# Cutting both tables' loads and the last two positions' stores by partition in a rotary-embedding kernel

## The chip, the cores and the metric

One Trainium2 chip, of which the kernel uses one core. The metric is the device time of one execution in microseconds (us). Before the change it is 163.35 us, the median of three runs that lie between 163.29 and 163.39 us.

## What is computed

The reference rotates pairs of numbers. `x` is float32 of shape (batch 8, positions 2048, heads 8, 64); `cos` and `sin` are float32 tables of shape (2048, 32), shared by all batches and heads:

```
x1, x2 = x[..., :32], x[..., 32:]
out1 = x1 * cos - x2 * sin
out2 = x1 * sin + x2 * cos
out  = concatenate([out1, out2], axis=-1)
```

The input and the output are 33.55 MB each, each table is 0.26 MB. Nothing is reduced, so every byte of `x` comes in once and every byte of `out` goes out once.

## The kernel before, in words

**Tiling.** The 2048 positions of a batch are laid on the 128 partitions, 16 consecutive positions on each. One position is HD = 8 x 64 = 512 numbers, that is 2 KB per partition; a batch is a tile `xt` of 128 rows by 8192 numbers (32 KB per row, 4 MB). A UNIT is four positions: 128 x 2048 numbers, 1 MB. The tables `cos_sb` and `sin_sb` are 128 rows of 512 numbers, 2 KB per row.

**Loads.** `load(b)` (lines 64 to 70) issues the loads of batch b on SyncE's queue (SP). Batch 0 comes in three parts (1, 1 and 2 MB), and right after the first part the cos table is loaded (line 69); every other batch is one 4 MB load. The sin table is loaded first of all on ScalarE's queue (ACT, line 76). Five tiles rotate (NBUF = 5): the loads of batches 0 to 4 are asked for at once, and batch b + 5 is loaded into the tile of batch b when that batch's stores have landed.

**Work.** `rotate(b, lo, n)` works on one piece, in place. In the commonest form ("A") GpSimd (POOL) multiplies the swapped halves by the sin table and by its negative `nsin` (line 122, two instructions), VectorE (DVE) multiplies by the cos table (line 129) and adds the two products back into `xt` (line 136). In five pieces of the run (kinds "B" and "C") TensorE adds the products through an identity matrix and ScalarE copies the sum back (lines 143 to 165). ScalarE makes `nsin` from the sin table once, after a table load of its own (line 90), and a copy of the sin table for "C" (line 91); VectorE copies the cos table once (line 93).

**Stores.** `store(b, lo, n)` (lines 72 to 74) writes a finished part out: on ACT's queue for batches 0 to 6 and on SP's for the last batch. `pieces(b)` (lines 170 to 175) gives the pieces of work, `shares(b)` (lines 177 to 182) the parts that are stored. The last batch is worked in three UNITs and two pieces of two positions each, and stored as 2 UNITs, 1 UNIT and 1 UNIT: the last store, 1 MB with rows of 8 KB, starts when the last piece is done.

**Order.** The order on each engine is the order of the program (`keep`). Every DMA signals on one of eight completion semaphores that are given out in turn, so a DMA that takes a semaphore up again waits first until that semaphore's DMA before it has landed. On the chip a DMA is carried by 16 DMA engines side by side; in the trace every DMA of this kernel has 16 landing marks, one for each of them, and it is complete with the last.

Of the kernel before, what the change touches and what calls it, by code (L numbers as in the profile page):

```python
# [10 lines left out]
def kernel(  # L11
# [7 lines left out]
    nc = tc.nc  # L19
    keep = tc.keep_in_program_order  # L20
# [5 lines left out]
    P = 128  # L26
    HD = H * D
    R = S // P
    ROW = R * HD
    UNIT = 4 * HD  # L30
    NBUF = 5
    C = 512
    last = B - 1

    xv = x.rearrange("b (q r) h d -> b q (r h d)", q=P)
    ov = out.rearrange("b (q r) h d -> b q (r h d)", q=P)
    cos_src = cos.rearrange("(q r) d -> q r d", q=P)
    sin_src = sin.rearrange("(q r) d -> q r d", q=P)
# [9 lines left out]
    cos_sb = const_pool.tile([P, R, Dh], f32, tag="cb")  # L48
    sin_sb = const_pool.tile([P, R, Dh], f32, tag="sb")
# [6 lines left out]
    xts = {}  # L56

    def spans(sizes):
        lo = 0
        for n in sizes:  # L60
            yield lo, n
            lo += n

    def load(b):
        xt = xpool.tile([P, ROW], f32, tag="xt", name=f"xt{b}")
        for lo, n in spans([UNIT, UNIT, 2 * UNIT] if b == 0 else [ROW]):
            keep(nc.sync.dma_start(out=xt[:, lo : lo + n], in_=xv[b, :, lo : lo + n]))
            if b == 0 and lo == 0:
                keep(nc.sync.dma_start(out=cos_sb, in_=cos_src))
        xts[b] = xt  # L70

    def store(b, lo, n):
        queue = nc.sync if b == last else nc.scalar
        keep(queue.dma_start(out=ov[b, :, lo : lo + n], in_=xts[b][:, lo : lo + n]))

    keep(nc.scalar.dma_start(out=sin_sb, in_=sin_src))
    for b in range(NBUF):
        load(b)

# [2 lines left out]
        out=eye,  # L82
        in_=eye,
# [93 lines left out]
    def shares(b):  # L177
        if b == 0:
            return [UNIT, UNIT, 2 * UNIT]
        if b == last:  # L180
            return [2 * UNIT, UNIT, UNIT]
        return [ROW]

    for b in range(B):
        done = 0
        outs = list(spans(shares(b)))
        for lo, n in spans(pieces(b)):
            rotate(b, lo, n)
            done = lo + n
            while outs and sum(outs[0]) <= done:  # L190
                store(b, *outs.pop(0))
        if b + NBUF <= last:
            load(b + NBUF)
# [30 lines left out]
```

## Time and profile before

| what | before |
|---|---|
| median of three runs | 163.35 us |
| the profiled execution, its own time | 163.35 us |
| its span, first to last instruction | 161.5 us |
| DVE busy | 140.1 us (87%) |
| POOL busy | 138.9 us (86%) |
| PE, PEld, ACT busy | 49.2, 18.5, 12.8 us |
| first packet of the first load begins | 1.75 us |
| first POOL product begins, first DVE product begins | 6.64 us, 7.79 us |
| last DVE sum ends | 152.2 us |
| last store issued, landed | 152.23 us, 160.71 us |
| bytes moved, mean rate over the span | 67.65 MB, 419 GB/s |
| DMA packets | 3458 |

Between the span and the execution's own time lie 1.85 us outside of the instructions. The busy shares are of the span. A "landing" is the moment at which the last of the 16 marks of a DMA is set. All times inside a run count from the span's start. The 40 digits of a row of the page stand for slices of 4.04 us.

### The profile page before, as it was taken

The page shows a single profiled execution, that of the slowest core. Times are in us where ns is not written, and L with a number is a line of the kernel's source. Part 1 is how long each engine was busy: PE and PEld are TensorE (multiplying, and loading weights), DVE is VectorE, ACT ScalarE, POOL GpSimd, SP SyncE. Part 2 cuts the span into 40 slices and gives each one's busy share as a digit, 9 for nine tenths or more (in the row PEclk, how much of TensorE's full clock was granted, in tenths as well). Part 3 has the DMA queues.
Part 4 walks back from the last instruction along what each step waited for, and adds up shares of the span by engine and source line. Part 5 has one row for each costly group of instructions (what it writes and reads, how often), then busy time and mean ns, then how long its engine had stood idle before and what let it go on. Part 6 is the DMA issues. An engine that isn't in the chain of part 4 may idle for free.

```text
span 161.5 us, 460 instructions
## 1 busy us (share of the span) xinstructions
PE 49.2 (30%) x80; PEld 18.5 (11%) x80; DVE 140.1 (87%) x66; ACT 12.8 (8%) x14; POOL 138.9 (86%) x70
## 2 busy tenths in 40 slices
PE   0000000597309770978039723973000000000000
PEld 0000000142004220323023302320000000000000
DVE  0297999999999999999999999999999999999600
ACT  3300000002200220021100220022000000000000
POOL 1399997999999999999994999999999999996000
PEclk9999999999975998589956995599655555555555
DMA  5999998998999999999999999999999999999994
GB/s 153 423 458 418 430 487 381 430 487 381 487 398 446 389 462 389 462 446 389 487 422 389 487 416 389 487 422 398 473 422 406 471 422 406 471 422 406 426 404 209
DMA packets 3458, 67.65 MB, mean 419 GB/s; under 512 B 384, under 2 KB 384, under 8 KB 640
## 3 DMA queue, kind: packets, MB, share of 16 engines
q1 hardware_dynamic: 2016, 38.01, 55.3%
q10 hardware_dynamic: 1440, 29.62, 42.8%
q14 instruction: 2, 0.02, 0.0%
HBM read 34.08 MB, written 33.55 MB: 419 GB/s over the span
## 4 chain that ended last, share of the span: by engine, by line
DVE 75%; POOL 9%; issue 6%; DMA 4%; DVEq 0%
DVE t L129 40%; DVE xt L136 33%; POOL t L122 9%; DMA sin_sb<-in_sin_dram 4%; DVE t L148 3%; DVEq L136 0%
## 5 line engine op out<-in xcount | busy, mean ns | idle before, releaser
L122 POOL TENSOR_TENSOR t<-xt,sin_sb 128x1024 f32<-128x1024 f32 (+1 forms) x32 | 71.2, 2226 | 8.5 <-DMA sin_sb<-in_sin_dram 5.3
L129 DVE TENSOR_TENSOR t<-xt,cos_ps 128x2048 f32<-128x2048 f32 (+1 forms) x34 | 73.4, 2166 | 0.8
L122 POOL TENSOR_TENSOR t<-xt,nsin 128x1024 f32<-128x1024 f32 (+1 forms) x32 | 71.3, 2228 | 0.0
L136 DVE TENSOR_TENSOR xt<-t,t 128x2048 f32<-128x2048 f32 (+1 forms) x29 | 62.2, 2145 | 4.2 <-POOL t L122 1.2
L143 PE MATMUL o<-t,eye 128*128 128x512 f32 x24 | 16.9, 797 | 23.1 <-DVE t L129 19.7
L160 PE MATMUL o<-t,eye 128*128 128x512 f32 x16 | 12.0, 842 | 37.9 <-DVE t L129 35.7
L144 PE MATMUL o<-t,eye 128*128 128x512 f32 x24 | 14.9, 709 | 0.0
L145 ACT COPY xt<-o 128x1024 f32<-128x1024 f32 x6 | 6.1, 1012 | 45.7 <-PE o L144 45.7
L143 PEld LDWEIGHTS o<-t,eye 128*128 128x128 f32 x24 | 5.5, 256 | 32.5 <-issue 26.6
L160 PEld LDWEIGHTS o<-t,eye 128*128 128x128 f32 x16 | 3.7, 256 | 43.4 <-issue 39.5
L165 ACT COPY xt<-o 128x1024 f32<-128x1024 f32 x4 | 4.0, 1012 | 47.8 <-PE o L161 47.8
L93 DVE COPY cos_ps<-cos_sb 128x512 f32<-128x512 f32 x1 | 0.7, 695 | 7.1 <-DMA cos_sb<-in_cos_dram 7.1
L144 PEld LDWEIGHTS o<-t,eye 128*128 128x128 f32 x24 | 5.6, 235 | 8.1 <-issue 8.1
L161 PE MATMUL o<-t,neye 128*128 128x512 f32 x8 | 6.2, 872 | 0.2
L148 DVE TENSOR_TENSOR t<-xt,sin_ps 128x2048 f32<-128x2048 f32 x2 | 4.6, 2280 | 0.0
L161 PE MATMUL o<-t,eye 128*128 128x512 f32 x8 | 4.1, 592 | 0.0
L161 PEld LDWEIGHTS o<-t,neye 128*128 128x128 f32 x8 | 2.1, 296 | 5.2 <-issue 3.6
L161 PEld LDWEIGHTS o<-t,eye 128*128 128x128 f32 x8 | 1.5, 190 | 1.9 <-issue 1.9
L90 ACT ACT_TABLE_LOAD x1 | 1.3, 1283 | 1.2 <-PEq L208 1.2
L90 ACT ACTIVATE nsin<-sin_sb 128x512 f32<-128x512 f32 x1 | 0.6, 630 | 4.1 <-DMA sin_sb<-in_sin_dram 4.1
L91 ACT COPY sin_ps<-sin_sb 128x512 f32<-128x512 f32 x1 | 0.6, 578 | 0.0
L80 POOL MEMSET eye<- 128x128 f32 x1 | 0.2, 204 | 0.3 <-POOLq L208 0.3
(6 smaller groups left out, 1.0 us busy)
## 6 DMA issues: line engine op xcount, KB each, us to landing
xt<-in_x_dram SPq DMA_DIRECT2D x7, 4096.0 KB, 34.5
out_dram<-xt ACTq DMA_DIRECT2D x6, 4096.0 KB, 30.5
xt<-in_x_dram SPq DMA_DIRECT2D x2, 1024.0 KB, 6.8
xt<-in_x_dram SPq DMA_DIRECT2D x1, 2048.0 KB, 12.3
out_dram<-xt ACTq DMA_DIRECT2D x2, 1024.0 KB, 19.3
out_dram<-xt ACTq DMA_DIRECT2D x1, 2048.0 KB, 28.0
out_dram<-xt SPq DMA_DIRECT2D x1, 2048.0 KB, 13.5
out_dram<-xt SPq DMA_DIRECT2D x2, 1024.0 KB, 9.9
```

What stands on the lines that cost most here:

```text
L90: keep(nc.scalar.mul(nsin, sin_sb, -1.0))
L93: keep(nc.vector.tensor_copy(cos_ps, cos_sb))
L122: nc.gpsimd.tensor_mul(out=t2u[:, :, u, :].rearrange("p (r h) d -> p r h d", h=H), in0=xu[:, :, 1 - u, :].rearrange("p (r h) d -> p r h d" ...
L129: nc.vector.tensor_mul(out=t1.rearrange("p (r k d) -> p r k d", r=nr, d=Dh), in0=xk, in1=rep(cos_ps[:, r0 : r0 + nr, :], 2 * H),)
L136: keep(nc.vector.tensor_add(out=xt, in0=t1, in1=t2))
L143: nc.tensor.matmul(oc, eye, t1[:, cs], start=True, stop=False)
L144: nc.tensor.matmul(oc, eye, t2[:, cs], start=False, stop=True)
L145: keep(nc.scalar.copy(xt[:, 2 * j * C : 2 * (j + 1) * C], o))
L148: nc.vector.tensor_mul(out=t2.rearrange("p (r k d) -> p r k d", r=nr, d=Dh), in0=xk, in1=rep(sin_ps[:, r0 : r0 + nr, :], 2 * H),)
L160: nc.tensor.matmul(oc, eye, t1u[:, gs, u, :], start=True, stop=False)
L161: nc.tensor.matmul(oc, eye if u else neye, t2u[:, gs, 1 - u, :], start=False, stop=True)
L165: nc.scalar.copy(xu[:, :, u, :], o.rearrange("p (g d) -> p g d", d=Dh))
```

## The change

Both tables' loads are each made by two DMAs, cut by partition: sin in rows 0 to 119 and 120 to 127, cos in rows 0 to 116 and 117 to 127. The last batch's last share of four positions is cut into three shares: two positions, one and one. The store of the last but one position (`lo` = 14 HD) is made by two DMAs of 126 and 2 rows, that of the last (`lo` = 15 HD) by two of 108 and 20 rows. The share of two positions ahead of them is complete one piece earlier than the others, and is stored then.

```diff
@@ load @@
             if b == 0 and lo == 0:
-                keep(nc.sync.dma_start(out=cos_sb, in_=cos_src))
+                for p in (slice(0, 117), slice(117, P)):
+                    keep(nc.sync.dma_start(out=cos_sb[p], in_=cos_src[p]))
@@ store @@
         queue = nc.sync if b == last else nc.scalar
-        keep(queue.dma_start(out=ov[b, :, lo : lo + n], in_=xts[b][:, lo : lo + n]))
-
-    keep(nc.scalar.dma_start(out=sin_sb, in_=sin_src))
+        rows = {(last, 14 * HD): 126, (last, 15 * HD): 108}.get((b, lo), P)
+        for p in (slice(0, rows), slice(rows, P)):
+            if p.start < P:
+                keep(queue.dma_start(out=ov[b, p, lo : lo + n], in_=xts[b][p, lo : lo + n]))
+
+    for p in (slice(0, 120), slice(120, P)):
+        keep(nc.scalar.dma_start(out=sin_sb[p], in_=sin_src[p]))
@@ shares @@
         if b == last:
-            return [2 * UNIT, UNIT, UNIT]
+            return [2 * UNIT, UNIT, 2 * HD, HD, HD]
```

In the built program SP issues 19 DMAs where it issued 14 (one more for cos, four more for the stores of the last batch), and ACT 11 where it issued 10. The instructions of DVE, POOL and PE are the same in the same order; only what some of them wait for differs.

## The prediction

> **What bounds the kernel now.** I read the page's slices and DMA queues first, then a table by stage, then the DMA records at the end.
>
> ```profile
> span 161.5 us, 460 instructions
> ...
> DMA  5999998998999999999999999999999999999994
> GB/s 153 423 458 418 430 487 381 430 487 381 487 398 446 389 462 389 462 446 389 487 422 389 487 416 389 487 422 398 473 422 406 471 422 406 471 422 406 426 404 209
> ...
> q1 hardware_dynamic: 2016, 38.01, 55.3%
> q10 hardware_dynamic: 1440, 29.62, 42.8%
> q14 instruction: 2, 0.02, 0.0%
> ```
>
> DVE is busy 87% and POOL 86%, but the DMA row is full from slice 2 to slice 39. The queues' shares add to 98.1% of 161.5 us: each of the 16 DMA engines carries 158.4 us of packets, and only 159.0 us lie between the first packet (1.75) and the last landing (160.71). The table by stage (us, five engines' busy time, granted clock, DMA share, GB/s) shows that the end belongs to the DMA engines:
>
> ```profile
> core 0: us, PE busy (x) PEld busy (x) DVE busy (x) ACT busy (x) POOL busy (x), PEclk, DMA share, GB/s
> ...
> 16.14:142.30 126.16, 49.24 (x80) 18.53 (x80) 122.72 (x54) 10.12 (x10) 123.01 (x54) 0.78 1.00 432
> 142.30:152.20 9.90, 0.00 (x0) 0.00 (x0) 9.49 (x6) 0.00 (x0) 5.72 (x5) 0.50 1.01 437
> 152.20:158.30 6.10, 0.00 (x0) 0.00 (x0) 0.00 (x1) 0.00 (x0) 0.00 (x0) 0.50 0.98 416
> 158.30:160.80 2.50, 0.00 (x0) 0.00 (x0) 0.00 (x0) 0.00 (x0) 0.00 (x0) 0.50 0.45 190
> ```
>
> DVE is done at 152.2 and the engines work off stores for 8.5 us more. The chain of waits ends at DVE's last sum, so it does not show this. The time is therefore start + the packets of the engine with the most to carry + tail, and the question is **which engine is last**. Two stretches at the end, same columns:
>
> ```profile
> 157.90:159.40 1.50, 0.00 (x0) 0.00 (x0) 0.00 (x0) 0.00 (x0) 0.00 (x0) 0.50 0.98 415
> ...
> 160.05:160.35 0.30, 0.00 (x0) 0.00 (x0) 0.00 (x0) 0.00 (x0) 0.00 (x0) 0.50 0.06 27
> ```
>
> The share 0.06 is one engine of 16, alone, at 27 GB/s. The 16 landing marks of the last store say the same: fourteen between 159.76 and 160.14, one at 160.37, one at 160.71 (mean 159.97). Going back over the stores, these two lags appear once each, after the only two packets that queue q14 (instruction code) moves inside the run: one at 94.09, one at 115.84.
>
> ```profile
> DMA packets 28, 0.47 MB, mean 934 GB/s; under 512 B 13, under 2 KB 13, under 8 KB 13
> ...
> q14 instruction: 1, 0.01, 3.9%
> ```
>
> (That is the answer for 94.0 to 94.5.) The first takes 0.309 us, and the neighbouring 32 KB packet 1.745 instead of 1.213: 0.84 us lost by one engine. The second costs 0.309 and 1.434 - 1.213: 0.53 us. No record names the engine.
>
> **The change, part by part.** *Prices.* The records last 0.084 us for a 2 KB row, 0.309 for 8 KB, and the next packet starts 0.004 earlier than the end, so 0.080 and 0.305; 4 KB lies between, by size 0.155. A completion mark costs 0.009.
>
> *Which engine carries which row.* In every DMA of before each engine has the same whole number of rows (8 of 128). No DMA of before has another number of rows, so this is bounded from two sides: rows spread over all 16 as evenly as they go (nothing moves: 0), or whole equal shares on as many engines as divide the rows. I take the second, since it is what all 24 DMAs show: 120 = 15 x 8 and 8 = 8 x 1; 117 = 13 x 9 and 11 = 11 x 1; 126 = 14 x 9 and 2 = 2 x 1; 108 = 12 x 9 and 20 = 10 x 2. I also take it that each split begins with the same engine; call them 0 to 15. [...]
>
> *Sum by engine.* Before, the four transfers are 8 + 8 rows of 2 KB and 8 of 8 KB (8 x 0.305 = 2.44 us). After, rows of 2 KB for the tables and the two last positions, and 8 x 0.155 = 1.24 us for the store ahead of them:
>
> - engines 0, 1: tables 9 + 10 rows (+3, +0.24); stores 1.24 + 21 x 0.080 = 2.92 (+0.48): **+0.72**
> - 2 to 7: +0.24; 1.24 + 20 x 0.080 = 2.84 (+0.40): **+0.64**
> - 8, 9: +0.16 + 0.40 = **+0.56**; 10: +0.16 + 0.24 = **+0.40**; 11: +0.08 + 0.24 = **+0.32**
> - 12: +0.08 - 0.48 = -0.40; 13: -0.64 - 0.48 = -1.12; 14: -0.64 - 1.20 = -1.84; 15: -1.28 - 1.20 = -2.48
>
> Up to five more completion marks add 0.02. So twelve engines gain 0.34 to 0.74 us (mean 0.63), four lose. What counts is on which side the engine at 160.71 stands.
>
> *Start.* The second cos DMA takes one more issue on SP (0.42 us, row of line 69), so the next loads start 0.5 later; the engines have the first load and the tables until their landings at 5.9 to 7.0, which covers it. By the order of semaphores the load of batch 1 (issued at 2.68) now waits for the first sin part (about 6.6); the 2 MB load ahead of it lands at 14.4, so 7 us of packets cover it. ScalarE's table load now waits for the second sin part:
>
> ```profile
> 1.16 1.28 ACT L90 ACT_TABLE_LOAD   x1 [1.16 <-PEq L208]
> 6.59 0.63 ACT L90 ACTIVATE nsin<-sin_sb 128x512 f32<-128x512 f32 x1 [4.15 <-DMA sin_sb<-in_sin_dram]
> ```
>
> It moves from 1.16 to about 6.6, `nsin` follows it (7.9 to 8.5), and POOL's second product, at 7.87 before, starts 0.7 later; with a landing of sin 0.1 to 0.3 later, 0.8 to 1.0. Behind it on ACT stand the sin copy and `neye`, first wanted at 30 us. POOL drives DVE until 16.14, so all computing shifts by 0.8 to 1.0. The cover is the queue of stores: the last store, issued at 152.23, had its packets begin at 157.9, and a DMA needs 1.0 us from issue to first packet (0.74 to 1.75), so it could come 4.7 us later. **Price nothing**; without the cover, up to 1.0.
>
> *End.* Four issues instead of one at 0.47 us each (SP's first loads: 1.17, 1.64, 2.10): the last at 153.2 + 1.4 = 154.6, still 2.3 early. The store of two positions is issued a piece earlier, behind the same queue: nothing. The DMAs of 126, 108 and 20 rows take up semaphores of the stores of batches 3, 4 and 5, landed at 114.8, 131.7 and 141.4: no wait. SP's last waits are seven instead of three, of which one comes after the last landing: 0 to 0.1.
>
> **Sum.** The engine at 160.71 gains 0.63 (0.34 to 0.74): 163.35 + 0.63 = **164.0 us**. The profiled execution and the median are both 163.35, so nothing is scaled.
>
> **Rivals.**
>
> 1. *Both late engines are among the four relieved* (on the other side: not slower). Then the last is one of the fourteen, of which the best placed end at 159.9 and the worst at 160.14, plus 0.64: 160.54 to 160.8 against 160.71. Time 163.15 to 163.5, middle 163.35. It decides as soon as both fetch lags sit in 12 to 15. Blind counting gives 5% (4/16 x 3/15); two packets of one queue may well use neighbouring engines, and of 15 neighbouring pairs three lie there, 20%. Two of the fourteen others also end apart, at 160.08 and 160.14, which would make four: I give 27%.
> 2. *Only the worse one is relieved.* Then the second decides: 160.37 + 0.34 to 0.74 = 160.7 to 161.1, middle 163.65. 10%, half on each side of the bound. [...]
> 3. *The short splits run slower per row*, because a share's rows no longer lie where that engine's rows lay. Nothing of before has such a share; the nearest slow 2 KB rows, among the first sin packets, took 0.23 to 0.53 us. At twice the price for the 20 rows of an ordinary engine's last stores: +1.6, 164.9; half of that, 164.2 to 164.8. 7%. [...]
> 4. *A shared ceiling*: relieving four engines lets the others run faster, and all end together near the mean, 159.97: 162.6. Against it: alone at the end, one engine moves 27 GB/s and its 8 KB packet still takes 0.309. 6%.
> 5. *The rows spread over all 16 anyway*: 163.3 to 163.5. 2%. *Odd row counts go to one or a few engines*: 117 rows on one engine are 9.4 us, 170 and more. 2%.
>
> **How the numbers follow.** Forecast 46%. A measurement of this kernel can tell about 0.2% (0.33 us) from no change. Slower: 46 + 5 + 7 + 2 = 60%. Same: 27 + 5 + 2 = 34%. Faster: 6%. The range takes in rivals 1, 2 and 5's first, and the lower part of 3: 163.15 to 164.45. The forecast's own range is 163.7 to 164.2.
>
> **What would show it.** Landing marks of the new DMAs: 15, 8, 13, 11, 14, 2, 12, 10 instead of 16 each. Marks of the last full store: four engines early by up to 1.3 us (tables alone), twelve later. The table load after 6.5 and DVE's end near 153, both without effect on the last landing. If the last landing stays near 160.7 and no single engine works alone, rival 1 holds; if 2 KB records of the last stores exceed 0.084, rival 3; if DMA engines stand idle before 152, my cover is wrong.

## The result, and the profile after

The changed kernel takes 165.39 us, the median of four runs between 165.16 and 165.72, against 163.37 us (163.29 to 163.41) before: the ratio is 1.0121, 95% interval 1.011 to 1.0133. It is slower by 2.0 us, where 0.63 us were forecast, and lies above the stated range. The profiled execution took 165.72 us, the longest of the four, 2.37 more than that of before; the numbers below are taken from it. Where runs of one kernel lie further apart than 1.5%, the times given are of those within 1.5% of its fastest.

The page of the changed kernel, its span, slices and DMA queues:

```profile
span 163.9 us, 468 instructions
...
DMA  5999999899999999999999999999999999999992
GB/s 157 312 442 440 412 436 496 380 410 490 392 448 416 432 488 400 408 480 392 456 440 400 480 402 432 456 392 480 402 432 456 400 480 408 424 448 404 406 387 99
...
q1 hardware_dynamic: 2318, 38.01, 55.1%
q10 hardware_dynamic: 1447, 29.62, 42.1%
q14 instruction: 2, 0.02, 0.0%
```

The DMA row is as full as before, and the bytes are the same. But 97.2% of 163.9 us is 159.3 us of packets per engine where it was 158.4: the same bytes took 0.9 us per engine longer. Slice 2 of the GB/s row shows where: 312 where it was 423, at the same nine tenths of busy time. The stretch from 3 to 12 us, first before and then after (columns as in the tables above; the last two are DMA share and GB/s):

```profile
3.00:4.00 1.00, 0.00 (x0) 0.00 (x0) 0.00 (x0) 0.00 (x0) 0.00 (x0) 1.00 0.99 322
4.00:5.00 1.00, 0.00 (x0) 0.00 (x0) 0.00 (x0) 0.00 (x0) 0.00 (x0) 1.00 0.92 385
5.00:8.00 3.00, 0.00 (x0) 0.00 (x0) 0.91 (x2) 1.35 (x3) 1.35 (x2) 1.00 1.04 425
8.00:12.00 4.00, 0.00 (x0) 0.00 (x0) 3.73 (x4) 0.00 (x0) 4.00 (x4) 1.00 1.06 453
```

```profile
3.00:4.00 1.00, 0.00 (x0) 0.00 (x0) 0.00 (x0) 0.00 (x0) 0.00 (x0) 1.00 0.86 301
4.00:5.00 1.00, 0.00 (x0) 0.00 (x0) 0.00 (x0) 0.00 (x0) 0.00 (x0) 1.00 0.97 385
5.00:8.00 3.00, 0.00 (x0) 0.00 (x0) 0.00 (x0) 0.35 (x1) 0.25 (x1) 1.00 1.07 291
8.00:12.00 4.00, 0.00 (x0) 0.00 (x0) 2.98 (x3) 2.28 (x4) 3.35 (x3) 1.00 1.03 426
```

From 5 to 8 us all engines are busy in both (1.04 and 1.07), yet they move 291 GB/s instead of 425: 3 us x 134 GB/s is 0.4 MB less, 0.9 us at the run's 433 GB/s. So **no engine waits; the packets themselves take longer**. In these 3 us the 2 KB packets of cos last 0.133 us on average instead of 0.084, and the 8 KB packets of batch 0, which the change does not touch, 0.465 instead of 0.310 (before 5 us they are alike, 0.393 and 0.392).

The end of the changed kernel, two rows of its tables by stage:

```profile
154.40:160.00 5.60, 0.00 (x0) 0.00 (x0) 0.00 (x0) 0.00 (x0) 0.00 (x0) 0.50 0.94 388
...
162.10:162.50 0.40, 0.00 (x0) 0.00 (x0) 0.00 (x0) 0.00 (x0) 0.00 (x0) 0.50 0.07 26
```

Again one engine works alone at the end (0.07 of 16, 26 GB/s). The landings show where the 2.37 us arose. The third load of batch 0 landed at 15.81 instead of 14.41 (+1.40). The last store that both kernels make alike, the 1 MB ahead of the last positions, landed at 159.57 instead of 158.29 (+1.28, so nothing was added in between). From there to the last landing it took 3.38 us (162.95) instead of 2.42 (+0.96). The rest, 0.13, lies behind the last landing.

### The profile page after: what moved, and what is told of

Read it like the earlier page. It is cut to its first block, busy times and chain, and to the rows that moved or that the text cites. A ratio compares the mean times of both kernels' runs of the same rounds, so it can differ in the third digit from the quotient of the medians.

```text
span 163.9 us, 468 instructions
## 1 busy us (share of the span) xinstructions
PE 50.1 (31%) x80; PEld 18.8 (11%) x80; DVE 140.1 (85%) x66; ACT 12.8 (8%) x14; POOL 138.9 (85%) x70
## 4 chain that ended last, share of the span: by engine, by line
DVE 74%; POOL 8%; issue 7%; DMA 4%; ACT 0%; ACTq 0%; DVEq 0%
DVE t L134 39%; DVE xt L141 32%; POOL t L127 8%; DMA sin_sb<-in_sin_dram 4%; DVE t L153 3%; ACTq L81 0%; ACT nsin L95 0%; DVEq L141 0%; ACT L95 0%; ACTq L95 0%
## 5 line engine op out<-in xcount | busy, mean ns | idle before, releaser
L127 POOL TENSOR_TENSOR t<-xt,nsin 128x1024 f32<-128x1024 f32 (+1 forms) x32 | 70.5, 2204 | 0.7 <-ACT nsin L95 0.7
L148 PE MATMUL o<-t,eye 128*128 128x512 f32 x24 | 17.4, 814 | 22.9 <-DVE t L134 19.5
L165 PE MATMUL o<-t,eye 128*128 128x512 f32 x16 | 12.2, 855 | 39.5 <-DVE t L134 37.3
L149 PE MATMUL o<-t,eye 128*128 128x512 f32 x24 | 14.9, 710 | 0.0
L166 PE MATMUL o<-t,eye 128*128 128x512 f32 x8 | 4.1, 592 | 0.0
```

What stands on the lines that cost most here:

```text
L127: nc.gpsimd.tensor_mul(out=t2u[:, :, u, :].rearrange("p (r h) d -> p r h d", h=H), in0=xu[:, :, 1 - u, :].rearrange("p (r h) d -> p r h d" ...
L148: nc.tensor.matmul(oc, eye, t1[:, cs], start=True, stop=False)
L149: nc.tensor.matmul(oc, eye, t2[:, cs], start=False, stop=True)
L165: nc.tensor.matmul(oc, eye, t1u[:, gs, u, :], start=True, stop=False)
L166: nc.tensor.matmul(oc, eye if u else neye, t2u[:, gs, 1 - u, :], start=False, stop=True)
```

## The experiments

The rivals: **A**, the prediction's, only the number of rows per engine counts; **B**, rows that are taken away from their usual engine slow both themselves and the packets beside them (the prediction's third rival; "B1" in the expectations, where "B2" is the form in which only the unequal use of engines costs); **C**, the cost lies in the extra DMAs, finer rows, issues and waits.

**The two halves of the change alone.** `e1_tables` keeps the stores of before, `e2_stores` the table loads of before.

> Only the tables' loads are split (120 + 8 and 117 + 11), the stores are those of before. Theory A, packet counts alone (the prediction's): engines that gain three table rows carry 0.24 us more, so 163.6 us. Theory B, splits whose shares are unequal or odd run slower at the start, for their own rows and for what runs beside them (in the changed kernel's trace the packets between 5 and 8 us took 1.05 us per engine longer than their usual length): 1.3 us more, 164.5 to 164.8. Theory C, the cost is at the end, in the stores: no more than 163.6 here.

> Only the last batch's stores are changed (shares of 2, 1 and 1 positions, 126 + 2 and 108 + 20 rows), the tables are loaded as before. Theory A: 0.40 to 0.48 us more, 163.8. Theory B: 0.85 more, 164.2 (sum of both parts as in the changed kernel). Theory C: nearly all of it, 165.0 or more.

Tables alone: 164.53 us, ratio 1.0072 (1.0057 to 1.0087), +1.2 us. Stores alone: 164.95, ratio 1.0096 (1.0073 to 1.0119), +1.6. Both are some three to five times what the counts give, so A's sizes fall in both places; theory C in the form "nearly all at the end" falls too. B's 164.2 for the stores was too low as well. The parts add to more than the whole (2.7 against 2.0). The tables-only kernel shows the same hole at the start, and the stores are as before:

```profile
5.00:8.00 3.00, 0.00 (x0) 0.00 (x0) 0.00 (x0) 0.41 (x1) 0.31 (x1) 1.00 1.06 290
```

In the stores-only kernel four 4 KB packets after 158 us lasted 0.391 to 0.648 us, where 0.159 is usual: the store of two positions, slowed while other engines already moved the cut rows.

**Finer stores without a cut by partition.**

```diff
-        rows = {(last, 14 * HD): 126, (last, 15 * HD): 108}.get((b, lo), P)
+        rows = P
```

> The last batch's shares are cut into 2, 1 and 1 positions, but each store has all 128 rows; tables as before. Counts: 8 rows of 8 KB at 0.305 become 8 of 4 KB at 0.155 and 16 of 2 KB at 0.080, 0.08 us more, and two more marks: 163.45. If finer rows and more DMAs by themselves are what slows the end: 163.8 or more.

163.6 us, ratio 1.002 (0.9995 to 1.0045; three of the ten runs took 164.35 to 164.87, as one of the kernel before beside them took 164.69): the finer rows and two more DMAs cost about what the counts say, and no 4 KB packet was longer than 0.159. So the cut by partition is what costs at the end.

**The same cuts, but with equal work for all engines.** 112 = 16 x 7 and 16 = 16 x 1, so by the author's counting each engine carries 8 rows as before, but, if the shares are consecutive rows, other ones (in `e9_allstores112` below, with nine stores cut so, 33 DMAs leave 528 mark packets, 16 each). `e4_tables112` cuts both tables so, `e7_stores112` both last positions:

```diff
-                for p in (slice(0, 117), slice(117, P)):
+                for p in (slice(0, 112), slice(112, P)):
...
-    for p in (slice(0, 120), slice(120, P)):
+    for p in (slice(0, 112), slice(112, P)):
```

> Both tables are split 112 + 16, stores as before: two DMAs each as in the change, but 16 engines with 7 + 1 rows, so every engine still carries 8 rows. Theory A: nothing, 163.35 to 163.45. A cost of two DMAs instead of one (issue, marks, waits): as much as with 120 + 8 and 117 + 11. Theory B in the form that unequal use of engines is what costs: 163.4; in the form that rows away from their usual engine cost: 164 or more.

> Tables as before; the last batch's stores as in the change, but both single positions are cut 112 + 16 instead of 126 + 2 and 108 + 20, so all 16 engines carry 7 + 1 rows of each. Counts: 0.08 us for the finer rows and a few marks, 163.5 to 163.6 as in the run with uncut rows. Theory B1, rows that lie away from their usual engine slow the packets beside them: 163.9 or more, with packets above their usual length at the end. Theory B2, only unequal use of engines costs: 163.6.

Tables: 163.9 us, ratio 1.003 (1.002 to 1.0039), with 347 GB/s between 5 and 8 us. Stores: 164.81, ratio 1.0113 (1.0043 to 1.0183), as much as with 126 + 2 and 108 + 20 (one of its four runs took 167.06, the others 164.66 to 164.94). Theory A gives 0.1 us or less for both. So unequal counts are not needed for the loss; for the tables they, or the odd shares, make up the rest of it (0.5 of 1.2 us without them).

**Two DMAs for each table, cut by columns.** Each of the two DMAs has all 128 rows (1 KB twice), so by the author's assumption every engine keeps its rows.

```diff
-                keep(nc.sync.dma_start(out=cos_sb, in_=cos_src))
+                for r in (slice(0, 8), slice(8, R)):
+                    keep(nc.sync.dma_start(out=cos_sb[:, r], in_=cos_src[:, r]))
```

> Each table is loaded by two DMAs that cut the columns (128 rows of 1 KB twice), so each engine keeps its own rows; stores as before. A price of two DMAs and of later waits (the second issue, the waits that move): 163.9, as with the tables cut 112 + 16. Theory B1: 163.4 to 163.5 (finer packets only, 16 of 1 KB for 8 of 2 KB, some 0.04 to 0.1 us a table).

163.5 us, ratio 0.9992 (0.9972 to 1.0012), and between 5 and 8 us:

```profile
5.00:8.00 3.00, 0.00 (x0) 0.00 (x0) 0.52 (x1) 0.71 (x1) 1.25 (x1) 1.00 1.05 413
```

413 GB/s beside 290: two DMAs, the second issue and the waits that move cost nothing. C falls for the tables.

**One table at a time.**

> Only sin is split (120 + 8). Counts: one row more for engines 0 to 7, 0.08 us. Theory B1: part of the 1.2 us that both tables cost together; beside the first load only, so 0.2 to 0.6: 163.6 to 164.0. ScalarE's table load still waits for it here, so if that is the cost it stays whole.

> Only cos is split (117 + 11). Counts: two rows more for engines 0 to 10, 0.16 us: 163.5. Theory B1: the larger part of the 1.2 us, 0.6 to 1.0 (the slow packets of the changed kernel lie between 5 and 8 us, beside cos): 164.0 to 164.4.

sin alone: 163.58, ratio 1.0015 (1.0006 to 1.0025). cos alone: 163.8, ratio 1.0025 (1.0016 to 1.0035), below what B was to give. The two together cost more (1.2 us) than one by one (0.2 + 0.4). The cos packets show whose price rises: with cos cut and sin whole they keep 0.084 us on average, and with sin cut and cos whole they take 0.113. So in these traces it is not a table's own cut that lengthens its rows, but the cut of the DMA beside it.

**The later computing.** The kernel before, with GpSimd's first product made three times:

```diff
-            for u, tab in ((1, sin_sb), (0, nsin)):
+            for u, tab in ((1, sin_sb),) * (3 if b == 0 and lo == 0 else 1) + ((0, nsin),):
```

> The kernel before, in which GpSimd does its very first product three times over, so that all computing starts some 2.4 us later, as the change moved it by 2.2 us. Step of the prediction that priced the later computing at nothing (the store queue hides up to 4.7 us): 163.35 to 163.5. Rival: the later computing is what moved the end: 165.4 or more.

163.33 us, ratio 0.9998 (0.9988 to 1.0007). Its timeline shows VectorE's last sum and the last store's issue:

```profile
153.37 1.22 DVE L136 TENSOR_TENSOR xt<-t,t 128x1024 f32<-128x1024 f32 x1
154.62 0.33 SPq L74 DMA_DIRECT2D out_dram<-xt  x1
```

The issue came 2.4 us later than before, and the last landing at 160.68 (160.71 before). The cover that the prediction named is there.

**The disputed cost made large.** If B holds, cutting all stores of batches 0 to 6 must cost much, with equal counts too. `e9_allstores112` cuts them 112 + 16, `e11_allstorescols` is the control by columns (seven eighths and one eighth), `e10_allstores64` cuts 64 + 64:

```diff
-        keep(queue.dma_start(out=ov[b, :, lo : lo + n], in_=xts[b][:, lo : lo + n]))
+        cut = 112 if b < last else P
+        for p in (slice(0, cut), slice(cut, P)):
+            if p.start < P:
+                keep(queue.dma_start(out=ov[b, p, lo : lo + n], in_=xts[b][p, lo : lo + n]))
```

> The tables and the last batch as before; every store of batches 0 to 6 is cut 112 + 16 by partition. Each engine carries 7 + 1 rows, so counts give marks only: 163.4. Theory B1: rows away from their usual engine slow the run over the whole length; the tables cut this way cost 0.5 us for 0.5 MB, so 29 MB could cost up to some 30 us; at least 166. If the slowing belongs to the start or to loads: 163.4 to 163.7.

> The control for the cut of all stores: every store of batches 0 to 6 is made by two DMAs, cut by columns at seven eighths, so every engine keeps its rows. One more packet per row (8 for each of 9 stores, 0.0045 us each) is 0.3 us: 163.7. If two DMAs for one slow the run by themselves, as much as with the cut by partition.

> Tables and last batch as before; every store of batches 0 to 6 is cut 64 + 64 by partition (16 engines, 4 + 4 rows). Theory B1 without more: slower by tens of us, as with 112 + 16 (196.0). If only a cut that leaves a remainder, or a small second part, is what costs, a clean half costs nothing: 163.5 to 164.

112 + 16: 193.7 us (193.19 and 194.3), ratio 1.1851 (1.1789 to 1.1913). 64 + 64: 194.2, ratio 1.1886 (1.1827 to 1.1944). By columns: 164.31, ratio 1.0041 (1.0018 to 1.0064), that is 0.7 us where the counts gave 0.3. So it is not the number of DMAs: a cut by partition with equal counts costs 30 to 31 us. The kernel with 64 + 64 by stage:

```profile
20.00:100.00 80.00, 39.98 (x65) 15.21 (x66) 78.24 (x36) 8.10 (x8) 76.79 (x35) 0.86 1.01 415
100.00:160.00 60.00, 9.16 (x16) 3.31 (x14) 49.98 (x24) 2.02 (x2) 47.96 (x23) 0.59 1.00 314
160.00:190.00 30.00, 0.00 (x0) 0.00 (x0) 0.00 (x0) 0.00 (x0) 0.00 (x0) 0.50 0.91 264
```

The engines stay busy (1.01, 1.00, 0.91) while the rate falls to 314 and 264 GB/s; before, it is 428 between 100 and 160 us. Its 32 KB store packets last 1.69 us on average (1.213 before), the uncut loads beside them 1.27.

**SBUF rows or DRAM rows, and loads.** `e13_loadshift` reads batches 0 to 6 from seven rows further on in DRAM without any cut (so it rotates other positions); `e14_allloads112` cuts the loads of batches 1 to 7; `e15_allstoresstep2` stores batches 0 to 6 in two halves of every second partition:

```diff
-        keep(queue.dma_start(out=ov[b, :, lo : lo + n], in_=xts[b][:, lo : lo + n]))
+        for p in (slice(0, P, 2), slice(1, P, 2)) if b < last else (slice(0, P),):
+            keep(queue.dma_start(out=ov[b, p, lo : lo + n], in_=xts[b][p, lo : lo + n]))
```

> The kernel before, but batches 0 to 6 load their 128 rows from seven rows further on in DRAM (so what it computes belongs to other positions: the input is shifted); the rows of SBUF are the usual ones and no DMA is cut. If the price hangs on which engine takes which DRAM row: slower, as the cut 112 + 16 shifts by one row per engine. If it hangs on the SBUF rows: 163.4.

> Tables, batch 0 and all stores as before; the loads of batches 1 to 7 are cut 112 + 16 by partition. If loads pay as stores do: 185 to 200, with packets of 32 KB well above 1.213 us. If only stores pay: under 166. (More DMAs wait for semaphores here, which may add a few us by itself; the length of the packets tells these apart.)

> Every store of batches 0 to 6 is made in two halves of 64 rows, every second partition each, where the run with 64 + 64 took rows 0 to 63 and 64 to 127 (194.2). If the loss comes from a half that reaches only a part of SBUF: well under 194, near 170. If it comes from an engine taking rows that are not its own in whatever order: 185 to 200 again.

Shifted DRAM rows: 164.23, ratio 1.0042 (1.0019 to 1.0065), with runs from 163.39 to 164.87; its 32 KB packets keep their length (1.213 and 1.223 us on average), so a shift of all 128 rows alike did not lengthen packets; where its 0.7 us come from was not followed (the kernel before took up to 164.28 beside it). Loads cut: 195.41 (one run), and in the profiled execution, which took 198.88, 32 KB load packets of 1.69 us on average: loads pay as stores do, though the waits that this kernel adds were not taken apart. Every second partition: 165.54, ratio 1.012 (1.007 to 1.0169), against 194.2 for two solid halves of the same size. By stage:

```profile
20.00:100.00 80.00, 38.22 (x65) 14.52 (x66) 78.24 (x36) 8.10 (x8) 76.84 (x35) 0.85 1.00 429
100.00:160.00 60.00, 9.10 (x16) 3.38 (x16) 50.29 (x24) 2.02 (x2) 48.20 (x23) 0.59 0.97 412
```

So what decides here is **which rows one DMA covers**, not how many DMAs or rows there are: 194.2 against 165.5 us, with two halves of 64 rows in both. Why the solid halves are the slow ones is in no record.

Two things are not shown. The halves of `e15_allstoresstep2` differ from those of `e10_allstores64` in DRAM as well as in SBUF, and the shift of `e13_loadshift` moved all rows of the loads alike, so a pattern of rows on the DRAM side is not excluded. And no record names the engine of a row, so the first reading in the expectation of `e15_allstoresstep2`, a half that reaches only a part of SBUF, is a conjecture that no run tells apart from B's "away from its usual engine". With 112 + 16, 262 of the 768 cut 32 KB packets are over 0.1 us too long, while the parts of 16 rows have only 96 packets: the parts of 112 rows, seven eighths of the partitions, pay too.

## Why the prediction was wrong, point by point

*The bound: right.* The DMA engines are full from slice 2 on, computing some 2.4 us later changed nothing (`e12_shift`), and the last engine alone sets the end.

*Which engine carries which row: right in the number of engines.* The new DMAs have 15, 8, 13, 11, 14, 2, 12 and 10 late landing marks; where there are fewer than 16, one more mark comes at once, 0.5 to 0.75 us after the issue. The cut tables leave three engines ahead: in the last 1 MB store they land at 157.4 to 157.7, the bulk at 158.2 to 158.7. That each split begins with the same engine, from which the prediction's sum by engine follows, was the author's assumption, and no run shows it: which row goes to which engine is in no record. What the runs show in its place, the numbers of late marks and the three engines ahead, fits it, and the prediction's own table, in which the tables relieve only 13, 14 and 15, and not the four of its last paragraph. The mean of its twelve gains is 0.61, not 0.63.

*On which side the late engines stand: right.* In the last DMA (20 rows, 10 engines) the late marks are at 162.00, 162.43 and 162.95 (three, where there were two). These engines are thus among the ten that the change loads most, and the 2-row DMA's two, at 160.75, are not late. Rival 1 and rival 2 fall. The lags come after the code packets again (97.71 and 117.08; the packets next to them took 1.844 and 1.522 us): one mark is late in the landing at 111.21, three in that at 130.56.

*Start: the hidden parts right, one part missing.* ScalarE's table load began at 7.65, after sin, as foretold, and the first products with it:

```profile
7.65 1.28 ACT L95 ACT_TABLE_LOAD   x1 [7.65 <-DMA sin_sb<-in_sin_dram]
7.75 1.25 POOL L127 TENSOR_TENSOR t<-xt,sin_sb 128x512 f32<-128x512 f32 x1 [6.44 <-DMA sin_sb<-in_sin_dram]
8.68 0.69 DVE L98 COPY cos_ps<-cos_sb 128x512 f32<-128x512 f32 x1 [8.68 <-DMA cos_sb<-in_cos_dram]
```

The first product with sin began 1.1 later, and sin landed 1.0 later (7.58), not 0.1 to 0.3; cos landed 1.5 later (8.58). Computing moved by 2.2, not 0.8 to 1.0. The cover of 4.7 us was enough.

*Prices: this is the step that failed.* "The records last 0.084 us for a 2 KB row, 0.309 for 8 KB ... so 0.080 and 0.305" was taken from DMAs of 128 rows, and held fixed beside cut ones: that a cut lengthens the packets of the DMAs that run with it was put at nothing. In the changed kernel cos rows took 0.133 on average and the untouched 8 KB packets beside them 0.465, where 0.084 and 0.310 are usual. At the start the counts give 0.24, measured was 1.40; the lengthened packets of cos (0.4 us per engine) and of the first two loads of batch 0 (0.385 instead of 0.342 over all 256, 0.7 us per engine) make up nearly all of the difference. At the end the counts give 0.40 to 0.48, measured 0.96. There three packets, 4 KB at 159.99 and 160.30 and 2 KB at 160.82, lasted 0.458, 0.444 and 0.236: 0.74 us over their usual length. The last engine's packets can be followed back by their starts and ends, and lead to those of 0.444 and 0.236: 0.44 over the usual length and 0.08 idle between them, together 0.52, the missing half. All other cut rows at the end kept 0.084, so here too it is not the price of a cut row as such.

*The rivals.* The third came nearest with 7% (rows that last longer), but put that on the last stores' own rows alone and stopped at 164.2 to 164.8 as its likely part; the larger half came at the start, on neighbours. Its sum also left out the counts: its 1.6 us come on top of the forecast's 164.0, which gives 165.6, and half of them 164.8. The runs with cut stores went its way (194.2 and 193.7 us), and no row of before spoke against it, so it deserved more than 7%. The fourth (a shared ceiling, faster) falls: the relieved engines ended early (157.4 to 157.7) and nothing sped up: of the 2 KB rows after 157 us none took less than 0.084 us, and an engine alone at the end moves 26 GB/s (27 before).

*What stays open.* Why the two tables together, or the two halves of the change, do not add up. In the stores-only kernel the lengthened 4 KB packets sum to 1.4 us over their usual length and in the whole change to 0.6; what makes that difference no run took apart. Open too is what makes a packet longer: the rows of SBUF that a DMA covers, the engine that carries a row, or the rows in DRAM. No version here beats the kernel before.

## What to carry to other kernels

In this kernel, whose DMA engines are the bound (share 1.00 from 16 to 142 us before), a cut by partition was no small matter (2.0 us for the change, 30 to 31 for 29 MB of stores). Count rows per engine, but first ask what the cut does to the packets that run beside it. If a transfer has to be cut, cut it by columns: the tables cut so cost nothing (0.9972 to 1.0012), 29 MB of stores 0.7 us. Here, the cuts that were to move rows between engines cost 2.0 us, more than the lags of 0.5 and 0.8 us that they could have evened out.

## What the runs showed of the hardware that was not expected

- Stores or loads of 29 MB cut 64 + 64 or 112 + 16 by partition make the kernel 30 to 32 us longer; with 64 + 64 the engines are busy for 0.91 of the time from 160 to 190 us and move 264 GB/s. Halves of every second partition cost 2 us.
- The loss falls on packets of other DMAs too: between 5 and 8 us uncut 8 KB loads last 0.465 instead of 0.310 us beside cut 2 KB rows, and uncut cos rows 0.113 instead of 0.084 beside cut sin rows.
- Two 8 KB code packets in the run delay one DMA engine each by 0.5 to 0.9 us, neighbouring packet included (0.84 and 0.53 before, 0.94 and 0.62 after). In the kernel before, one landing mark is late from the landing at 109.91 on and a second from that at 129.30 on, and both still are at the last landing.
